# S5 mixer in channel-major form: 32-column output matmuls, half swaps and shifts as ACT copies, no folding transfers

## The chip, the core and the metric

The kernel runs on one core of a Trainium2 chip. Its engines are PE (TensorE, matrix products into PSUM; PEld in the profile is its weight load), DVE (VectorE, elementwise work), ACT (ScalarE, activations and copies), POOL (GpSimd) and SP (whose queue issues nearly all DMAs). The metric is the time of one execution in microseconds (us), the median of the runs. Lower is better.

## What is computed

Four layers on a 256 x 1024 activation: an even layer (stick-breaking attention and an S5 mixer, side by side), a gated linear attention layer, and two hybrid layers. The change touches the S5 mixer of the even layer alone:

```python
def s5_mixer(u, lam_re, lam_im, log_dt, b_re, b_im, c_re, c_im, d_skip, w_glu, b_glu):
    uf = u.reshape(bsz, L, S5_GROUPS, S5_GROUP)          # 32 groups of 16 channels
    lam_bar = exp(lam * dt)                              # 64 complex states a group
    b_bar = ((lam_bar - 1.0) / lam)[..., None] * bmat
    bu = einsum('gnp,blgp->blgn', b_bar, uf)             # complex
    h[t] = lam_bar * h[t - 1] + bu[t]                    # by associative_scan
    y = einsum('gpn,blgn->blgp', c_re, h.real) - einsum('gpn,blgn->blgp', c_im, h.imag) + d_skip * uf
    y = gelu(y.reshape(bsz, L, S5_WIDTH))
    return y * sigmoid(y @ w_glu + b_glu)
```

## The kernel before

Weights stream from HBM in 1 MB tiles (`Prog.loads`, raw, three buffers). ACT rounds each tile to an fp32r part (`highs`, whi), DVE makes the remainder (`lows`, wlo, four instructions of 512 columns a tile), and PE multiplies with both (`proj_a`, tile pa; `proj_b`, tile pb). whi and wlo have three buffers each, so DVE can run up to three tiles ahead of PE.

The order of the instructions on every engine is fixed when the program is built. Each part of the work is a generator, a fiber (`Prog.spawn`), and `Prog.run` takes again and again the fiber whose next instruction can start first by the planner's own table of costs (`Engine.__getattr__`) and a bias. On the chip each engine then works through its list in that order.

Even layer (`even_layer`): PE does the projections q, u, k, v, q, k, v, then z_b (ezb, two tiles), z_a (eza, four), the gate of the S5 mixer (eglu, `glu_evac`), and the output projection (eout, `out_proj`). `stick_fiber` (attention, PSUM tile sbz) and `s5_fiber` run beside them. The S5 mixer works on time in blocks: four steps are one block, so 64 blocks j of four steps t, and eight groups of 16 channels are one piece, so four pieces b. In `s5_piece`, piece by piece:

- ep: four transposes turn the table ez (made on DVE by `s5_tables`) into weights, which ACT copies to E twice, once with each of two 16-channel masks (g.half).
- inner: gp is a small product for the response within a block, G its masked form; four products with the shift matrices sh1 to sh3 and the identity shift G down by 32 partitions a step into tp, which ACT copies to Tt (s5T).
- vp: eight products of E with the input U; ACT copies vp to V. A product with the matrix jt swaps the halves of V (real and imaginary parts, with a sign) into jp. DVE turns V by the angles of the tables cosj and sinj, scans it, turns it back; the second turn has another product with jt.
- yp: per quarter q one product Tt[q] x U and two products F x m, which go to PSUM partitions 0 to 63 and 64 to 127. Rows of yp are (pair, step t, channel). ACT copies yp to Y.

All PE products of the S5 mixer are plain float32; the profile shows two records for each, one for each of its two passes. After the fourth piece `s5_fiber` folds Y into channel-major order with 32 DMAs on SP's queue (s_room<-s5Y), adds d_skip * u, and makes the gelu with ACT and DVE; y2 is split into the tile mix (`y_split`), which eglu reads. The input u is folded by 16 DMAs (s_room<-s_room, `u_evac`).

All instructions are emitted by one helper, so every line of the profile says L275; tiles are told apart by name. s_room is the shared tile that holds cosj, sinj, U and u.

Of the kernel before, what the change touches and what calls it, by code (L numbers as in the profile page):

```python
# [87 lines left out]
for _n, _w in _COLS:  # L88
# [4 lines left out]
    ["ident", "ones", "negtri", "negones", "mlt", "mneg", "cum", "mle", "jt", "misc", "sh1", "sh2", "sh3"])}  # L93
# [3 lines left out]
def _consts():  # L97
    i = np.arange(P)
    s, t = i[:, None], i[None, :]
    c = np.zeros((P, 13, P), np.float32)  # L100
# [8 lines left out]
    for m in range(64):  # L109
        c[m + 64, 8, m] = -1  # L110
        c[m, 8, m + 64] = 1
    c[:, 9, :64] = np.arange(64)
    c[:, 9, 65:] = 1
    for n in range(3):
        c[:, 10 + n] = s == t + 32 * (n + 1)
# [145 lines left out]
class Engine:  # L261
# [604 lines left out]
def program(g):  # L866
# [13 lines left out]
    c3 = A["cst"].rearrange("p (a b) -> p a b", a=13)  # L880
# [13 lines left out]
    def later():  # L894
        yield lambda: "later" in g.flags
        yield sp.dma_start(out=sgc, in_=A["cst2"][:, 1792:1796])
        yield sp.dma_start(out=g.cst1, in_=c3[:, 2:13, :])
        yield sp.dma_start(out=g.rsin.bitcast(I32), in_=A["pos"].to_broadcast([P, T]))
# [22 lines left out]
    with tc.tile_pool(name="blk1", bufs=1) as blk1:  # L921
        g.cst1 = blk1.tile([P, 11, P], F32, name="cst1")
# [157 lines left out]
def s5_tables(g, S):  # L1080

    act, dve, pool = g.act, g.dve, g.pool
    for b in range(4):
# [19 lines left out]
        own = lambda t: lambda a: t.rearrange("p (q a t c) -> p q a t c", q=4, t=4, a=2)[:, :, a]  # L1103
        F = yield from g.get("s5F", [P, 512])
        yield from s5_tab(g, bc, own(F), S.L[:, 0, gs, :], 2)
        yield from s5_tab(g, bc, own(m), S.L[:, 1, gs, :], 3)
        yield dve.tensor_tensor(F, F, m, op=OP.subtract)
        g.put(m, bc)
        S.fr[b] = (F, rho)


def s5_piece(g, S, Y, b):

# [11 lines left out]
    E = yield from g.get("s5E", [P, 4, 2, P])  # L1125
# [4 lines left out]
    Tt = yield from g.get("s5T", [P, 4, P])  # L1130

    def inner():
# [7 lines left out]
        tp = yield from g.ps1("proj", "s5tp")  # L1140
        tp4 = tp.rearrange("p (x t c) -> p x t c", x=8, t=4)
# [3 lines left out]
        g.put(tp, f0)  # L1145
# [6 lines left out]
    g.put(E)  # L1152
    if b == 3:
        g.flags.add("E")
    V = yield from g.get("s5V", [P, 512])
    yield act.activation(V, vp, AF.Copy)
    g.put(vp)
    jp = yield from g.ps1("small", "s5jp")
    yield pe.matmul(jp, g.K("jt"), V, start=True, stop=True)
# [5 lines left out]
    yield dve.tensor_tensor(r3(B)[:, :, 1:64], cb[:, :, 1:64], r3(V)[:, :, 0:63], op=OP.mult)  # L1165
    m = yield from g.get("s5m", [P, 512])
    yield dve.tensor_tensor(r3(m)[:, :, 1:64], sb[:, :, 1:64], r3(jp)[:, :, 0:63], op=OP.mult)
    g.put(jp)
    yield dve.tensor_tensor(r3(B)[:, :, 1:64], r3(B)[:, :, 1:64], r3(m)[:, :, 1:64], op=OP.subtract)
    if b not in S.fr:  # L1170
        yield lambda: b in S.fr
    F, rho = S.fr[b]
# [19 lines left out]
    g.put(F, m, Tt)  # L1192
    yield act.activation(Y[:, 4 * b:4 * b + 4, :], yp[:, 0:256].rearrange("p (q j) -> p q j", q=4), AF.Copy)
# [3 lines left out]
def s5_fiber(g, S):  # L1197
    act, dve, pool, sp, C = g.act, g.dve, g.pool, g.sp, g.C
    uT = S.uT
    Y = yield from g.get("s5Y", [P, 16, 64])  # L1200
    for b in range(4):
        yield from s5_piece(g, S, Y, b)

    yT = S.U.rearrange("p (b t) j -> p b t j", b=4)
    Y4 = Y.rearrange("p (b q) j -> p b q j", b=4)
# [10 lines left out]
    yf = S.U.rearrange("p b j -> p (b j)")
    for b in range(4):
        yb = yT[:, b].rearrange("p t j -> p (t j)")
        c = slice(b * T, (b + 1) * T)
        yield dve.scalar_tensor_tensor(yb, uT[:, b].rearrange("p t j -> p (t j)"), C("s5d", b), yb, op0=OP.mult, op1=OP.add)  # L1220
        yield act.activation(sq[:, c], yf[:, c], AF.Square)
    for h in range(2):
        c = slice(h * 512, (h + 1) * 512)
        yield dve.tensor_scalar(sq[:, c], sq[:, c], 0.044715, 1.0, op0=OP.mult, op1=OP.add)
        yield dve.tensor_tensor(gi[:, c], sq[:, c], yf[:, c], op=OP.mult)
        yield act.activation(gi[:, c], gi[:, c], AF.Tanh, scale=math.sqrt(2.0 / math.pi))

    for b in range(4):
        yield dve.scalar_tensor_tensor(y2[:, b].rearrange("p (j t) -> p t j", t=4),
                                       gi[:, b * T:(b + 1) * T].rearrange("p (t j) -> p t j", t=4),  # L1230
                                       1.0, yT[:, b], op0=OP.add, op1=OP.mult)
    g.put(S.room)
    g.flags.add("y2")
# [49 lines left out]
def even_layer(g, ev):  # L1283
# [723 lines left out]
```

## Time and profile before

| | |
|---|---|
| median of 3 runs | 1039.59 us (1039.35 to 1040.86) |
| profiled execution | 1040.25 us, span 1038.5 us |
| PE busy | 1016.1 us (98%) |
| DVE busy | 822.6 us (79%) |
| ACT busy | 564.4 us (54%) |
| granted TensorE clock | 0.998 of full |
| S5 pieces on PE | from 60.9 to 138.6 us |
| DMA, mean | 185 GB/s |

The span is cut in stretches with the view of windows; waits are read in the view of who waited for whom; prices of single steps are distances of starts in the timeline, since neighbouring matmuls overlap. A busy time is a union: the gap of a matmul's fill and drain is hidden in it.

### The profile page before, as it was taken

The page shows a single profiled execution, that of the slowest core. Times are in us where ns is not written, and L with a number is a line of the kernel's source. Part 1 is how long each engine was busy: PE and PEld are TensorE (multiplying, and loading weights), DVE is VectorE, ACT ScalarE, POOL GpSimd, SP SyncE. Part 2 cuts the span into 40 slices and gives each one's busy share as a digit, 9 for nine tenths or more (in the row PEclk, how much of TensorE's full clock was granted, in tenths as well). Part 3 has the DMA queues.
Part 4 walks back from the last instruction along what each step waited for, and adds up shares of the span by engine and source line. Part 5 has one row for each costly group of instructions (what it writes and reads, how often), then busy time and mean ns, then how long its engine had stood idle before and what let it go on. Part 6 is the DMA issues. An engine that isn't in the chain of part 4 may idle for free.

```text
span 1038.5 us, 14764 instructions
## 1 busy us (share of the span) xinstructions
PE 1016.1 (98%) x5507; PEld 857.5 (83%) x5507; DVE 822.6 (79%) x1855; ACT 564.4 (54%) x957; POOL 1.7 (0%) x15
## 2 busy tenths in 40 slices
PE   9999999899999999999999999999999999999996
PEld 7877888687887788888888888878888888888885
DVE  7998958777889777775799987775776759996775
ACT  6658667455744754544534564565454453365552
POOL 0000000000000000000000000000000000000000
PEclk9999999999999999999999999999999999999999
DMA  8543142545647486563533666544645454354541
GB/s 318 196 137 132 51 135 89 203 162 213 262 180 263 178 318 267 204 243 122 186 139 125 230 254 243 197 150 181 243 167 218 163 172 157 124 197 169 202 176 41
DMA packets 33491, 192.35 MB, mean 185 GB/s; under 512 B 8171, under 2 KB 9195, under 8 KB 11148
## 3 DMA queue, kind: packets, MB, share of 16 engines
q1 hardware_dynamic: 33132, 190.90, 51.2%
q8 instruction: 43, 0.70, 0.3%
q10 hardware_dynamic: 288, 0.52, 0.1%
q14 instruction: 28, 0.23, 0.1%
HBM read 189.31 MB, written 1.05 MB: 183 GB/s over the span
## 4 chain that ended last, share of the span: by engine, by line
PE 78%; DVE 13%; DMA 3%; ACT 2%; issue 2%; SPq 0%; DVEq 0%; ACTq 0%
PE pb L275 47%; PE pa L275 19%; DVE wlo L275 4%; PE as L275 3%; PE ret L275 2%; DMA raw<-in_wall_dram 2%; PE sbz L275 1%; DVE rs L275 1%; ACT whi L275 1%; DVE s5B L275 1%; PE s5yp L275 1%; PE gsc L275 1%; DVE s_room L275 1%; DMA cols<-in_cols_dram 1%; DVE H L275 0%
## 5 line engine op out<-in xcount | busy, mean ns | idle before, releaser
L275 PE MATMUL pb<-H,whi 128*128 128x512 f32 x1344 | 470.3, 401 | 1.2 <-ACT qsq L275 0.8
L275 DVE TENSOR_TENSOR wlo<-raw,whi 128x512 fp32r<-128x512 f32 x604 | 393.0, 687 | 93.2 <-ACT whi L275 93.2
L275 PE MATMUL pb<-H,wlo 128*128 128x256 f32 x1344 | 353.6, 283 | 0.0
L275 ACT ACTIVATE whi<-raw 128x1024 fp32r<-128x1024 f32 x302 | 304.6, 1052 | 69.2 <-PE pa L275 33.0
L275 PEld LDWEIGHTS pb<-H,whi 128*128 128x128 f32 x1344 | 242.6, 188 | 47.8 <-issue 1.5
L275 PEld LDWEIGHTS pb<-H,wlo 128*128 128x128 f32 x1344 | 253.5, 189 | 15.9 <-issue 0.7
L275 PE MATMUL pa<-whi,H 128*128 128x512 f32 x576 | 181.8, 394 | 2.1 <-DVE H L275 2.1
L275 PEld LDWEIGHTS pa<-whi,H 128*128 128x128 f32 x576 | 107.3, 188 | 26.2 <-DVE H L275 3.5
L275 PE MATMUL pa<-wlo,H 128*128 128x512 f32 x288 | 113.8, 395 | 0.0
L275 ACT ACTIVATE zz<-pb 128x256 f32<-128x256 f32 x120 | 45.0, 379 | 115.8 <-PE pb L275 115.2
L275 PE MATMUL pb<-yy,whi 128*128 128x512 f32 x192 | 67.6, 399 | 0.2
L275 DVE TENSOR_TENSOR zz<-pb,zz 128x256 f32<-128x256 f32 x120 | 49.8, 421 | 19.7 <-ACT zz L275 19.2
L275 DVE SCALAR_TENSOR_TENSOR acc<-raw,cact,acc 128x512 f32<-128x512 f32 x84 | 60.0, 747 | 4.6 <-DMA raw<-in_wall_dram 4.6
L275 PEld LDWEIGHTS pa<-wlo,H 128*128 128x128 f32 x288 | 54.1, 188 | 11.5 <-DVE wlo L275 0.3
L275 PE MATMUL pb<-yy,wlo 128*128 128x256 f32 x192 | 48.7, 281 | 0.0
L275 PE MATMUL pa<-whi,mg 128*128 128x512 f32 (+1 forms) x144 | 41.3, 369 | 0.0
L275 PEld LDWEIGHTS pb<-yy,whi 128*128 128x128 f32 x192 | 34.8, 188 | 7.3 <-DVE tg L275 1.5
L275 PEld LDWEIGHTS pb<-yy,wlo 128*128 128x128 f32 x192 | 36.2, 189 | 2.8
L275 PE MATMUL pa<-whi,mix 128*128 128x512 f32 x96 | 30.3, 393 | 3.0 <-ACT mix L275 2.3
L275 ACT ACTIVATE sqj<-x 128x512 f32<-128x512 f32 (+1 forms) x19 | 11.5, 606 | 37.1 <-DVE x L275 32.6
L275 PEld LDWEIGHTS pa<-whi,mg 128*128 128x128 f32 x144 | 26.0, 188 | 5.1
L275 ACT ACTIVATE ka<-pb 128x256 f32<-128x256 f32 x24 | 9.2, 385 | 37.4 <-PE pb L275 37.4
(289 smaller groups left out, 1142.7 us busy)
## 6 DMA issues: line engine op xcount, KB each, us to landing
raw<-in_wall_dram SPq DMA_DIRECT2D x174, 1024.0 KB, 4.8
x<-in_x_dram SPq DMA_DIRECT2D x2, 512.0 KB, 5.5
raw<-in_wall_dram SPq DMA_DIRECT2D x2, 512.0 KB, 5.8
s5bc<-in_s5bc_dram SPq DMA_DIRECT2D x4, 256.0 KB, 2.6
gate<-in_bgate_dram SPq DMA_DIRECT2D x2, 512.0 KB, 5.9
c<-in_cst_dram SPq DMA_DIRECT2D x1, 896.0 KB, 6.5
cst<-in_cst_dram SPq DMA_DIRECT2D x1, 704.0 KB, 11.7
s_room<-s_room SPq DMA_DIRECT2D x16, 32.0 KB, 4.5
```

Of the source, the lines that this page charges most:

```text
L275: i.eng, i.emit = name, (lambda: real(*a, **k))
```

## The change

- Outputs channel-major: for each step t the piece makes rows (quarter q, channel) of yp, 32 partitions for each q. Tt and F are padded with zeros to 32 columns (two groups of 16) and live in two fixed tiles S.Tt (s_T in the rows) and S.F (s_F), cleared once by POOL. The 12 matmuls of a piece become 48 of 128 x 32 weights and 64 columns, four neighbours writing to the four quarters of the PSUM partitions. Writers of both tiles wait for the flag ("yp", b - 1), set when the matmuls of the piece before are issued.
- Y, its four ACT copies and the 32 DMAs go; d_skip * u is added by DVE straight out of yp, per piece.
- The halves are swapped by two ACT copies of 64 partitions each (`turned`) instead of the product with jt; V is then the swapped copy and DVE reads vp itself.
- The shifts of G are six ACT copies (one of 128, one of 64 and four of 32 partitions, 128 columns each) instead of the four products with sh1 to sh3 and the identity and the copy of 512 columns. The constants jt, sh1, sh2, sh3 go: the second load of constants is 448 KB instead of 704 KB.
- Paired inputs: ACT masks U (two copies of 256 columns into EU) instead of E, and vp is four products with 128 columns instead of eight with 64.
- The subtraction that ends F is two instructions of 256 columns instead of one of 512.
- The gelu is made in two halves; the first half is a fiber of its own that starts in the fourth piece. y2 takes the buffer of E, z_b that of Y.
- The planner books 0.04 us for a matmul with an output of 32 partitions.

```diff
@@ cost table
                     i.cost = (0.4167 * n + 13.4) * 1e-3 if rhs.dtype == F32R else max(0.224, (1.667 * n + 4) * 1e-3)
+                    if chip[0][1].shape[0] == 32:
+                        i.cost = 0.04
@@ s5_tables
+        if b:
+            yield lambda: ("yp", b - 1) in g.flags
+        F = lambda a: S.F[:, :, a, :, 16 * a:16 * a + 16]
+        own = lambda a: m.rearrange("p (a q t c) -> p a q t c", q=4, t=4, a=2)[:, a]
...
-        yield dve.tensor_tensor(F, F, m, op=OP.subtract)
+        for a in range(2):
+            yield dve.tensor_tensor(F(a), F(a), own(a), op=OP.subtract)
@@ s5_piece
-    for a in range(2):
-        yield act.activation(E[:, :, a, :], ep.rearrange("p (q n) -> p q n", q=4), AF.Copy,
-                             scale=g.half[:, a:a + 1])
+    yield act.activation(EU[:, 0, :], ep, AF.Copy)
...
-        for tau in range(4):
-            yield pe.matmul(tp4[:, :, tau, :], g.K(f"sh{3 - tau}") if tau < 3 else g.ident, G, start=True, stop=True)
-        yield act.activation(Tt, tp.rearrange("p (q n) -> p q n", q=4), AF.Copy)
+        if b:
+            yield lambda: ("yp", b - 1) in g.flags
+        for tau, p0, n in ((3, 0, 128), (2, 32, 32), (2, 64, 32), (2, 96, 32), (1, 64, 64), (0, 96, 32)):
+            d = p0 - 32 * (3 - tau)
+            yield act.activation(Tt[d:d + n, :, tau, :], G3[p0:p0 + n], AF.Copy)
...
-    for i in range(8):
-        yield pe.matmul(vp[:, i * 64:(i + 1) * 64], E[:, i // 2, i % 2, :], U[:, 4 * b + i // 2, :], start=True, stop=True)
+    for a in range(2):
+        yield act.activation(EU[:, 1].rearrange("p (q a j) -> p q a j", q=4, a=2)[:, :, a, :], U[:, 4 * b:4 * b + 4, :], AF.Copy,
+                             scale=g.half[:, a:a + 1])
+    for q in range(4):
+        yield pe.matmul(vp[:, q * P:(q + 1) * P], EU[:, 0, q * P:(q + 1) * P], EU[:, 1, q * P:(q + 1) * P], start=True, stop=True)
...
+    def turned(o, v):
+        yield act.activation(o[0:64], v[64:128], AF.Copy, scale=-1.0)
+        yield act.activation(o[64:128], v[0:64], AF.Copy)
-    yield act.activation(V, vp, AF.Copy)
-    yield pe.matmul(jp, g.K("jt"), V, start=True, stop=True)
+    yield from turned(V, vp)
...
-    yield pe.matmul(jp, g.K("jt"), V, start=True, stop=True)
-    yield dve.tensor_tensor(m, jp, m, op=OP.add)
+    yield from turned(m, V)
+    yield dve.tensor_tensor(r3(B), cb, r3(B), op=OP.mult)
+    yield dve.tensor_tensor(m, m, B, op=OP.add)
...
-    for q in range(4):
-        yield pe.matmul(yp[:, q * 64:(q + 1) * 64], Tt[:, q, :], U[:, 4 * b + q, :], start=True, stop=False,
-                        skip_group_check=True)
+    for t in range(4):
+        o = lambda q: yp[32 * q:32 * q + 32, t * 64:(t + 1) * 64]
+        for q in range(4):
+            yield pe.matmul(o(q), Tt[:, q, t, :], U[:, 4 * b + q, :], start=True, stop=False, skip_group_check=True)
         for a in range(2):
-            i = 2 * q + a
-            yield pe.matmul(yp[64 * a:64 * a + 64, q * 64:(q + 1) * 64], F[:, i * 64:(i + 1) * 64], m[:, i * 64:(i + 1) * 64],
-                            start=False, stop=a == 1, skip_group_check=True)
-    yield act.activation(Y[:, 4 * b:4 * b + 4, :], yp[:, 0:256].rearrange("p (q j) -> p q j", q=4), AF.Copy)
+            for q in range(4):
+                i = 2 * q + a
+                yield pe.matmul(o(q), S.F[:, q, a, t, :], m[:, i * 64:(i + 1) * 64], start=False, stop=a == 1, skip_group_check=True)
+    g.flags.add(("yp", b))
+    yield dve.scalar_tensor_tensor(yb, S.uT[:, b].rearrange("p t j -> p (t j)"), g.C("s5d", b), yp[:, 0:T], op0=OP.mult, op1=OP.add)
@@ s5_fiber
-    for q in range(4):
-        for a in range(2):
-            for t in range(4):
-                yield (g.pool if t == 9 else sp).dma_start(out=yT[(2 * q + a) * 16:(2 * q + a) * 16 + 16, :, t, :],
-                                                        in_=Y4[a * 64 + t * 16:a * 64 + t * 16 + 16, :, q, :])
+    yield from gelu(1)
+    yield from g.join(S.first)
```

How the lists move, at three places. First PE, the output matmuls of piece 0 (s5T, s_T: response within a block; s5F, s_F: output table). Before:

```order
L275 MATMUL qtp<-cst_76,qraw 128x128
L275 MATMUL s5yp<-s_room,s5T 128x64
L275 MATMUL s5yp<-s5m,s5F 64x64 x2
L275 MATMUL s5yp<-s_room,s5T 128x64
L275 MATMUL s5yp<-s5m,s5F 64x64 x2
```

After:

```order
L269 MATMUL s5yp<-s_room,s_T 32x64 x4
L269 MATMUL pa<-wlo,H 128x512
L269 MATMUL pa<-whi,H 128x512
L269 MATMUL s5yp<-s5m,s_F 32x64 x8
L269 MATMUL s5yp<-s_room,s_T 32x64 x4
L269 MATMUL s5yp<-s5m,s_F 32x64 x8
```

The pair "one full-width, two half-width" comes four times before; now four rounds of four and eight quarter-width matmuls, with other matmuls put in behind the first four (so in pieces 0, 1 and 3; piece 2 has none).

Second ACT, between the first vp and the next table (s5E now holds EU; s5f is G and later the next f0). Before:

```order
L275 ACTIVATE s5E<-s5ep,sgc 128x4x128
L275 ACTIVATE vE<-pa 128x512
L275 ACTIVATE s5V<-s5vp 128x512
L275 ACTIVATE s5T<-s5tp 128x512
L275 ACTIVATE s5f_845<-s5bc,sgc 128x128
```

After:

```order
L269 ACTIVATE s5E<-s5ep 128x512
L269 ACTIVATE s5E<-s_room,sgc 128x4x64 x2
L269 ACTIVATE vE<-pa 128x512
L269 ACTIVATE s_T<-s5f_162 128x4x32
L269 ACTIVATE s5V<-s5vp 64x512 x2
L269 ACTIVATE s_T<-s5f_162 32x4x32 x3
L269 ACTIVATE s_T<-s5f_162 64x4x32
L269 ACTIVATE s_T<-s5f_162 32x4x32
L269 ACTIVATE s5f_840<-s5bc,sgc 128x128
```

The four S5 copies up to G (the first of E stands two rows higher) have become eleven. Over the whole list ACT has 33 instructions more, three of them loads of an activation table (14 instead of 11).

Third DVE, from the sum out of the last yp to the first part of mix that eglu reads. After the change:

```order
L269 SCALAR_TENSOR_TENSOR s_room<-s_room,cols,s5yp 128x256
L269 TENSOR_TENSOR zz<-pb,zz 128x256
L269 TENSOR_TENSOR wlo<-raw,whi 128x512
L269 TENSOR_SCALAR s_room<-s_room 128x512
...
L269 TENSOR_TENSOR wlo<-raw,whi 128x512 x3
L269 TENSOR_TENSOR zz<-pb,zz 128x256
L269 SCALAR_TENSOR_TENSOR y_1654<-s_room 128x4x64 x2
L269 TENSOR_TENSOR gz<-gz,oT 128x512 x2
L269 SCALAR_TENSOR_TENSOR mix<-y_1654,mix 128x256
```

From that sum to the fourth `mix<-y` the list has 30 DVE instructions. On PE the last yp stood before the z_b tiles, in the last v projection; now piece 2 stands among the z_b tiles and piece 3 in the z_a tiles, 34 pb pairs, 6 sbz products with constants and 12 with vE before the first eglu matmul. DVE's list up to the last `mix<-glt` of the even layer is four instructions longer and has as many `wlo` as before (96); the lists of the layers behind it are the same on PE.

## Rows read from the trace of the kernel before

**Rows 1.** Page, part 1: busy time and share of the span, instructions

```profile
PE 1016.1 (98%) x5507; PEld 857.5 (83%) x5507; DVE 822.6 (79%) x1855; ACT 564.4 (54%) x957; POOL 1.7 (0%) x15
```

**Rows 2.** Windows: length, busy per engine (x instructions), clock, DMA share, GB/s

```profile
57.44:203.00 145.56, 139.98 (x816) 113.45 (x814) 124.73 (x270) 98.81 (x181) 1.28 (x8) 1.00 0.38 128
188.00:203.00 15.00, 11.18 (x48) 8.22 (x48) 13.55 (x24) 7.98 (x16) 0.61 (x2) 1.00 0.64 230
203.00:230.00 27.00, 26.59 (x121) 21.73 (x121) 17.05 (x37) 14.27 (x22) 0.00 (x0) 1.00 0.34 123
```

**Rows 3.** Waits of PE, 57.44 to 230: total, times, longest

```profile
PE pa L275 <- ACT mix L275: 2.3, 1, 2.3
PE pb L275 <- DVE zz L275: 1.1, 2, 0.7
```

**Rows 4.** Timeline of PE: start, us, instructions; first vp, swap and shifts

```profile
64.78 2.00 PE L275 MATMUL s5vp<-s_room,s5E 128*128 128x64 f32 x16
66.61 0.36 PE L275 MATMUL s5gp<-s5f,s5ez 128*128 128x32 f32 x2
...
67.59 1.02 PE L275 MATMUL s5jp<-s5V,cst 128*128 128x512 f32 x2
68.44 1.05 PE L275 MATMUL s5tp<-s5f,cst 128*128 128x128 f32 x8
69.25 0.47 PE L275 MATMUL pa<-wlo,H 128*128 128x512 f32 x1
```

**Rows 5.** Timeline of PE, the first yp

```profile
77.63 0.35 PE L275 MATMUL s5yp<-s_room,s5T 128*128 128x64 f32 x2
77.91 0.34 PE L275 MATMUL s5yp<-s5m,s5F 128*64 128x64 f32 x4
78.17 0.43 PE L275 MATMUL s5yp<-s_room,s5T 128*128 128x64 f32 x2
...
80.06 0.55 PE L275 MATMUL qtp<-cst,qraw 128*128 128x128 f32 x3
```

**Rows 6.** Weight loads of the first yp: tile view (min/median/max ns), then timeline

```profile
L275 PEld LDWEIGHTS s5yp<-s5m,s5F x64: 132/134/136, 77.9 to 138.3; 128*64 128x64 f32 x64
...
77.90 0.20 PEld L275 LDWEIGHTS s5yp<-s5m,s5F 128*64 128x64 f32 x4
...
78.17 0.30 PEld L275 LDWEIGHTS s5yp<-s_room,s5T 128*128 128x128 f32 x2
```

**Rows 7.** Waits of DVE, 57.44 to 203

```profile
DVE wlo L275 <- ACT whi L275: 6.2, 4, 4.5
DVE zz L275 <- ACT zz L275: 5.9, 2, 3.4
...
DVE s5m L275 <- PE s5jp L275: 1.5, 3, 0.6
```

**Rows 8.** Tile view of F: DVE instructions

```profile
L275 DVE TENSOR_TENSOR s5F<-s_L,s5bc x8: 418/430/468, 61.7 to 124.0; 128x256 f32<-128x256 f32 x8
L275 DVE TENSOR_TENSOR s5F<-s5F,s5t x4: 682/700/735, 65.5 to 125.6; 128x512 f32<-128x512 f32 x4
```

**Rows 9.** The start: ACT in the timeline, and the load of constants

```profile
26.43 2.01 ACT L275 ACTIVATE whi<-raw 128x1024 fp32r<-128x1024 f32 x2 [0.81 <-DMA raw<-in_wall_dram]
...
cst<-in_cst_dram SPq DMA_DIRECT2D x1, 704.0 KB, 11.7
```

**Rows 10.** ACT: the copy of vp (tile view), the table load (group, mean ns)

```profile
L275 ACT ACTIVATE s5V<-s5vp x4: 585/594/598, 66.8 to 127.6; 128x512 f32<-128x512 f32 x4
...
L275 ACT ACT_TABLE_LOAD x11 | 14.1, 1283 | 0.9 <-PEq L1997 0.7
```

**Rows 11.** Chain that ended last, in order of time: stretches of PE

```profile
103.49 3.60 PE sbz L275 x12
...
108.60 2.73 PE sbz L275 x24
...
144.67 9.04 PE pb L275 x51
```

More of the change, by code (lines that the diff above doesn't have):

```diff
@@ L92 @@
 CST = {n: i for i, n in enumerate(
-    ["ident", "ones", "negtri", "negones", "mlt", "mneg", "cum", "mle", "jt", "misc", "sh1", "sh2", "sh3"])}
+    ["ident", "ones", "negtri", "negones", "mlt", "mneg", "cum", "mle", "misc"])}
 def _consts():
@@ L108, in _consts @@
     c[:, 7] = s <= t
[L109 to L115, printed above, removed]
+    c[:, 8, :64] = np.arange(64)
     c2 = np.zeros((P, 1796), np.float32)
@@ L896, in later @@
         yield sp.dma_start(out=sgc, in_=A["cst2"][:, 1792:1796])
-        yield sp.dma_start(out=g.cst1, in_=c3[:, 2:13, :])
+        yield sp.dma_start(out=g.cst1, in_=c3[:, 2:9, :])
         yield sp.dma_start(out=g.rsin.bitcast(I32), in_=A["pos"].to_broadcast([P, T]))
@@ L1148, in s5_piece @@
         yield g.on("u")
+    for a in range(2):
+        yield act.activation(EU[:, 1].rearrange("p (q a j) -> p q a j", q=4, a=2)[:, :, a, :], U[:, 4 * b:4 * b + 4, :], AF.Copy,
+                             scale=g.half[:, a:a + 1])
     vp = yield from g.ps1("small", "s5vp")
-    for i in range(8):
-        yield pe.matmul(vp[:, i * 64:(i + 1) * 64], E[:, i // 2, i % 2, :], U[:, 4 * b + i // 2, :], start=True, stop=True)
-    g.put(E)
+    for q in range(4):
+        yield pe.matmul(vp[:, q * P:(q + 1) * P], EU[:, 0, q * P:(q + 1) * P], EU[:, 1, q * P:(q + 1) * P], start=True, stop=True)
+    g.put(EU)
     if b == 3:
-        g.flags.add("E")
+        S.y2 = yield from g.get("s5E", [P, 4, T], name="y2")
+        S.first = g.spawn(S.gelu(0), 0.1)
+    def turned(o, v):
+        yield act.activation(o[0:64], v[64:128], AF.Copy, scale=-1.0)
+        yield act.activation(o[64:128], v[0:64], AF.Copy)
     V = yield from g.get("s5V", [P, 512])
-    yield act.activation(V, vp, AF.Copy)
-    g.put(vp)
-    jp = yield from g.ps1("small", "s5jp")
-    yield pe.matmul(jp, g.K("jt"), V, start=True, stop=True)
+    yield from turned(V, vp)
     cb, sb = S.cosj[:, gs, :], S.sinj[:, gs, :]
@@ L1164, in s5_piece @@
     yield pool.memset(r3(B)[:, :, 0:1], 0.0)
[L1165 to L1169, printed above, removed]
+    yield dve.tensor_tensor(r3(B)[:, :, 1:64], cb[:, :, 1:64], r3(vp)[:, :, 0:63], op=OP.mult)
+    g.put(vp)
+    yield dve.tensor_tensor(r3(V)[:, :, 0:63], sb[:, :, 1:64], r3(V)[:, :, 0:63], op=OP.mult)
+    yield dve.tensor_tensor(r3(B)[:, :, 1:64], r3(B)[:, :, 1:64], r3(V)[:, :, 0:63], op=OP.subtract)
     if b not in S.fr:
         yield lambda: b in S.fr
-    F, rho = S.fr[b]
+    rho = S.fr[b]
     yield dve.tensor_tensor_scan(B, rho.rearrange("p a j -> p (a j)"), B, 0.0, OP.mult, OP.add)
@@ L1175, in s5_piece @@
     yield dve.tensor_tensor(r3(V), sb, r3(B), op=OP.mult)
-    yield dve.tensor_tensor(r3(m), cb, r3(B), op=OP.mult)
-    g.put(B)
-    jp = yield from g.ps1("small", "s5jp")
-    yield pe.matmul(jp, g.K("jt"), V, start=True, stop=True)
-    g.put(V)
-    yield dve.tensor_tensor(m, jp, m, op=OP.add)
-    g.put(jp)
+    m = yield from g.get("s5m", [P, 512])
+    yield from turned(m, V)
+    yield dve.tensor_tensor(r3(B), cb, r3(B), op=OP.mult)
+    g.put(V)
+    yield dve.tensor_tensor(m, m, B, op=OP.add)
@@ L1216, in s5_fiber @@
[L1216 to L1231, printed above, removed]
+    act, dve = g.act, g.dve
+    gw = S.cosj.rearrange("p a j -> p (a j)")
+    yf = S.U.rearrange("p b j -> p (b j)")
+    def gelu(h):
+        y2 = S.y2
+        sq, gi = gw[:, 1024 * h:1024 * h + 512], gw[:, 1024 * h + 512:1024 * h + 1024]
+        y = yf[:, 512 * h:512 * h + 512]
+        yield act.activation(sq, y, AF.Square)
+        yield dve.tensor_scalar(sq, sq, 0.044715, 1.0, op0=OP.mult, op1=OP.add)
+        yield dve.tensor_tensor(gi, sq, y, op=OP.mult)
+        yield act.activation(gi, gi, AF.Tanh, scale=math.sqrt(2.0 / math.pi))
+        for b in range(2):
+            c = slice(b * T, (b + 1) * T)
+            yield dve.scalar_tensor_tensor(y2[:, 2 * h + b].rearrange("p (j t) -> p t j", t=4), gi[:, c].rearrange("p (t j) -> p t j", t=4),
+                                           1.0, y[:, c].rearrange("p (t j) -> p t j", t=4), op0=OP.add, op1=OP.mult)
@@ L1232, in s5_fiber @@
+    S.gelu = gelu
+    for b in range(4):
+        yield from s5_piece(g, S, b)
+    yield from gelu(1)
+    yield from g.join(S.first)
     g.put(S.room)
@@ L1409, in even_layer @@
             sticks.append(g.spawn(stick_fiber(g, qk, oT, hf, pr), -0.05))
-    if "E" not in g.flags:
-        yield g.on("E")
-    zb = yield from g.get("s5E", [P, 4, T], name="zb")
+    zb = yield from g.get("s5Y", [P, 4, T], name="zb")
     for j in range(2):
```

45 lines of the change are left out of this document (18 added, 27 removed).

## The prediction

> **What bounds the kernel now.** I read the page's busy times first: PE is busy 98% of the span, DVE 79%, ACT 54% [rows 1]. So time taken from PE counts, as long as another engine doesn't step into its place. That has to be read from the stretch of the S5 mixer, not from the mean, so the windows come second. From the first S5 table on DVE (57.44 us) to DVE's last product for the gate of the S5 mixer (203.0) the stretch is 145.56 us long; PE is busy for 139.98 of it, DVE for 124.73, ACT for 98.81 [rows 2]. PE is ahead by 15 us only, much less than on the page. The waits of PE come third: it loses 5.6 us in the stretch (145.56 - 139.98), of which 2.3 and 1.1 are its two largest waits, at the end, for parts of mix and for zz [rows 3]. In the last 15 us before 203 DVE is busy for 13.55, PE for 11.18 only [rows 2]. DVE is the next bound, and the end of this layer already belongs to it. Behind 203 PE is busy for 26.59 of 27 us and DVE for 17.05 [rows 2]; what is gained at 203 should reach the end, where PE's list is the same.
>
> **PE, piece by piece.** Prices are distances of starts.
> - The two products with jt: the first takes 67.59 to 68.44, 0.85 us [rows 4]. Two a piece: -1.70.
> - The shifts: 68.44 to 69.25, -0.81 [rows 4].
> - vp: 16 records from 64.78 to 66.61, 1.83 us [rows 4]. It becomes 8 records with full-width weights and 128 columns, the form of the shifts, whose 8 records take 0.81: -1.02.
> - yp: 24 records from 77.63 to 80.06, 2.43 us [rows 5]. It becomes 96 records, that is 12 sets of four matmuls that write to four different quarters. No row shows a set, so I bound it. Below: 512 columns passed twice take 0.85 us [rows 4], so 64 columns twice take 0.11, and four side by side no less: 12 x 0.11 = 1.3 us. Above, as long as they run in twos like the half-width ones: two of those take 0.26 (77.91 to 78.17), a change of width there and back with it [rows 5], so 24 x 0.26 = 6.2 us. I take 0.15 a set, near the low end: the four half-width loads of two matmuls last 0.20 us together and 0.134 each, so the last begins 0.07 behind the first, where two full-width loads (0.30 together) begin 0.11 apart [rows 6]. Neighbours in different columns run side by side, and within the new loop the width doesn't change. That is 1.8. One change of width there and back is added: a quarter of the old loop lasts 0.61, of which two full-width records are 0.23 (1.83 / 8) and two half-width matmuls side by side 0.11, which leaves 0.27. In all 2.1: -0.3.
>
> Together -3.83 a piece, -15.3 for four. In three pieces the order puts other matmuls in behind the first four of yp: three more changes of width, +0.8. PE: **-14.5**, to 125.5 us in the stretch. The transposes and gp stay.
>
> The Trainium skill (TensorEngine Tiling, Instruction Overhead) speaks against small pieces: each matmul carries some 60 cycles, so that few columns cost as much as 60, and the gain of tiling shouldn't be taken from a dimension that is small already. By that, at the 2.4 GHz that the granted clock of 1.00 means, an estimate from the page is 96 x 0.025 = 2.4 us of overhead a piece, 2.7 with the change of width, and PE would gain 12.1 instead of 14.5. The half-width loads of rows 6, four begun in 0.07 us, speak for less than that.
>
> **DVE** does the same work: turn, scan and sums keep count and size, d_skip and gelu too. Only the end of F is cut: two of 430 ns for one of 700 [rows 8], +0.16 a piece, +0.6, so 125.4 us. So DVE stands level with PE, and the sum goes by DVE: 125.4 us and its waits. It has 20.8 us without work now (145.56 - 124.73). Of these, 6.2 and 5.9 are waits for whi and zz [rows 7]: whi had no free buffer and zz no finished product, so PE's pace made them, and a faster PE takes them away. Of the other 8.7, the 1.5 for the product with jt [rows 7] go. I keep 7 for what is left: sbz, tables, and now ACT's swaps. Stretch: 125.4 + 7 = 132.4 instead of 145.56, **-13.2**. The bounds are 0 us of waits (-20.2) and 12 (-8.2). PE then waits some 7 us in the stretch, mostly late.
>
> **ACT** gets more: per piece 13 copies instead of five, none longer than the 594 ns of a 512-column copy from PSUM [rows 10], so below +5 us a piece, and three table loads of 1283 ns [rows 10], +3.9. Even that bound makes 98.8 + 24 = 123 us, below 132. As work it is hidden by PE and DVE; without that cover it would cost those 24 us. As a wait it counts: DVE and PE stand behind each swap, and a swap can stand behind a pair of whi (2.01 us, rows 9). That is in the 7.
>
> **Edits that cost nothing.** The 32 DMAs of Y and its four copies (ACT) go from a tail that PE covers with the z projections. SP issues its weight loads without them in between; no wait of PE names them. POOL's two clears come before any table, on an engine with 1.7 us of work [rows 1]. The flags "yp" change little: the old single buffers of F and Tt made the same wait.
>
> **The start.** The load of constants falls from 704 KB [rows 9] to 448. Weight tiles queue behind it, and ACT waits 0.81 us for one at 26.43 [rows 9]. A gain between 0 and 0.8; I take **-0.2**, since DVE is busy soon after whatever PE does.
>
> **Sum.** -13.2 - 0.2 = -13.4 us against the profiled execution's own 1040.25: 1026.9. That execution stands 0.7 above the median of the runs (1039.59), so I forecast **1026** for the median. With DVE's bounds this case runs from 1019 to 1031.
>
> **Rivals.**
> 1. *The S5 chain comes too late for its gate.* Pieces 2 and 3 have moved from the v projections to the z tiles. Between the last yp and eglu PE has 34 pairs of pb (68 records; 51 take 9.04, so 12.1) and sbz of 3.60 and 2.73 [rows 11], 18.4 us. DVE has 30 instructions there, at the pace of the last 15 us (13.55 / 24, rows 2) 16.9 us. So only 1.5 us are free: what DVE is behind PE at the last yp beyond that, PE waits before eglu. For it: the two are level in the sum. Against it: eglu starts with the first quarter of mix. If DVE's waits are 13 instead of 7, the gain is 7.4 and the time about 1032; the case runs from 1031 to 1036.
> 2. *PE can't begin records fast enough (the other side).* Place: yp. The old loop's 24 records in 2.43 us are 0.10 each [rows 5]; if no stream goes faster, 96 records are 9.7 us, 10.0 with the change of width, +7.6 instead of -0.3, so +4.0 a piece and +16: PE's stretch 156 and its 5.6 of waits, **1055**. It decides from (2.43 + 3.53 - 0.27) / 96 = 0.059 us a record: above that the change loses on PE. For it: no stretch of records in rows 4 and 5 is denser than 0.10. Against it: four loads begun in 0.07 us [rows 6].
> 3. *The same, at the break-even*: about 0.06 a record, PE is even and the time stays near 1039. The Trainium skill has a figure for that (TensorE: Matmul & The Clock Gate, "Wait — 56ns, not 53.3ns?"): 62 ns for each matmul that the sequencer decodes in its own code, which binds where the array's work is shorter. Whether it binds here no row shows: all streams in the rows have longer work.
>
> That the change doesn't do what it says is out: the order has no jp, tp or Y left and 48 quarter-width matmuls a piece.
>
> **Chances.** Forecast 0.61, late chain 0.27, break-even 0.06, slower 0.06. A measurement of this kernel tells 0.2%, about 2 us. Faster is 0.61 + 0.27 = 0.88, same 0.06, slower 0.06. The range from 1020 to 1035 leaves out the last two (0.12) and thin ends of the first two. It takes in DVE's waits from 1 to 10 us and the late chain nearly whole.
>
> **What would show it.** A yp of about 2 us, up to 2.7 at the skill's estimate, would bear the price out; above 5.7 a piece refutes it. From DVE's first table to its last `mix<-glt` I expect 132 us, DVE over 93% busy, PE near 125. PE's waits should be at eglu and in the output projection, 7 us together; over 12 before eglu is rival 1. Behind that the two traces should run in step, 13 us apart. If DVE's waits fall on swaps (ACT) instead, the copies were too cheap in my sum. The forecast is wrong if DVE's share stays near 86% while PE's falls.

## The result, and the profile after

The changed kernel takes **1027.66 us** (median of 4 runs, 1025.53 to 1028.51); the kernel before takes 1040.01 in the same comparison (4 runs, 1039.35 to 1040.86). The ratio is 0.9878, 95% interval 0.9860 to 0.9895: 12.4 us faster, forecast 1026. The profiled execution of the changed kernel is its fastest, 1025.53 us, span 1023.7, so the two traces stand 14.8 us apart, 2.4 more than the medians. One of the six executions of the run with more matmuls behind yp (below) ran at a granted clock of 0.849 and took 1106.43 us; its median is given without that one.

The page's busy times after, against [rows 1]:

```profile
PE 998.8 (98%) x5715; PEld 846.2 (83%) x5715; DVE 823.6 (80%) x1859; ACT 581.0 (57%) x990; POOL 3.0 (0%) x17
```

PE has 17.3 us less work, DVE 1 more, ACT 16.6 more; PE's idle time has grown from 22.4 us (1038.5 - 1016.1) to 24.9. The windows after: the stretch of the prediction (first table on DVE to its last `mix<-glt`), its last 15 us, and the 27 us behind it, with the columns of [rows 2]:

```profile
55.99:186.84 130.85, 121.88 (x1016) 101.33 (x1015) 124.66 (x274) 114.30 (x214) 1.29 (x8) 0.99 0.38 134
171.84:186.84 15.00, 11.27 (x48) 9.10 (x47) 13.81 (x24) 10.27 (x18) 0.61 (x2) 0.89 0.39 144
186.84:214.00 27.16, 26.75 (x122) 21.90 (x121) 15.85 (x37) 13.39 (x22) 0.00 (x0) 1.00 0.42 155
```

The stretch is 14.7 us shorter. DVE is busy for 95% of it (before 86%), PE for 121.88 us, ACT for 114.30. The waits of PE after, from the first table to 214 us, against [rows 3]:

```profile
PE pb L269 <- DVE zz L269: 3.7, 1, 3.7
PE sbz L269 <- ACT sb_sp L269: 1.1, 1, 1.1
PE s5yp L269 <- ACT s_T L269: 1.1, 1, 1.1
PE sbz L269 <- DVE sb_sp L269: 0.9, 1, 0.9
PE s5yp L269 <- DVE s5m L269: 0.8, 2, 0.4
```

The largest lies in the gate of the S5 mixer. Two timelines show it, PE and then DVE:

```profile
173.87 0.40 PE L269 MATMUL pb<-mix,whi 128*128 128x512 f32 x1
178.00 0.50 PE L269 MATMUL pb<-mix,whi 128*128 128x512 f32 x1 [3.73 <-DVE zz L269]
...
180.08 0.63 PE L269 MATMUL pa<-whi,mix 128*128 128x512 f32 x1
180.51 0.63 PE L269 MATMUL pa<-wlo,mix 128*128 128x512 f32 x1
...
182.21 0.62 PE L269 MATMUL pa<-whi,mix 128*128 128x512 f32 x2
182.67 0.40 PE L269 MATMUL pa<-wlo,mix 128*128 128x512 f32 x1
```

```profile
170.90 3.09 DVE L269 TENSOR_TENSOR wlo<-raw,whi 128x512 fp32r<-128x512 f32 x5
174.19 0.69 DVE L269 SCALAR_TENSOR_TENSOR gz<-gz,zz 128x512 f32<-128x512 f32 x1 [0.20 <-ACT gz L269]
...
177.52 1.08 DVE L269 TENSOR_TENSOR zz<-pb,zz 128x256 f32<-128x256 f32 x3
```

PE wants a PSUM buffer at 174.3 us; DVE frees it with the zz at 177.52. Before that DVE had spent 3.09 us on five remainders for the output projection, which starts at 180. But they don't hold it up: behind them it still waits 0.20 us for gz from ACT. ACT's timeline shows why that gz is late:

```profile
169.93 0.39 ACT L269 ACTIVATE zz<-pb 128x256 f32<-128x256 f32 x1 [0.40 <-PE pb L269]
170.21 2.00 ACT L269 ACTIVATE whi<-raw 128x1024 fp32r<-128x1024 f32 x2
172.23 1.28 ACT L269 ACT_TABLE_LOAD   x1
173.53 0.64 ACT L269 ACTIVATE gz<-zz 128x512 f32<-128x512 f32 x1
```

Between the zz of the z_a tiles and gz stand two roundings for the output projection and the load of an activation table. From gz to the zz that frees the buffer, DVE and ACT take turns. So the wait belongs to both lists.

The wait costs more than itself. Windows of the 3.5 us behind it and of the next 3.8:

```profile
178.69:182.21 3.52, 3.52 (x11) 2.85 (x10) 2.75 (x5) 2.27 (x5) 0.00 (x0) 0.52 0.01 5
182.21:186.00 3.79, 3.79 (x18) 3.12 (x17) 3.79 (x7) 2.23 (x4) 0.30 (x1) 1.00 0.00 0
```

After PE stood still for 3.73 us its granted clock is 0.52, the 1.2 GHz level, and a matmul of 512 columns takes 0.43 us (180.08 to 180.51); at 1.00 it takes 0.23 (two from 182.21 to 182.67). For the ten that begin in the stretch, seven of 512 and three of 256 columns, that is an estimated 1.5 us more, which the page books as busy.

The new operations. PE's timeline of piece 2, whose yp nothing interrupts, and of the first vp; then ACT's copies in the tile view (min/median/max ns):

```profile
63.13 1.05 PE L269 MATMUL s5vp<-s5E 128*128 128x128 f32 x8
63.94 0.47 PE L269 MATMUL pa<-wlo,H 128*128 128x512 f32 x1
...
129.00 0.32 PE L269 MATMUL s5yp<-s_room,s_T 128*32 128x64 f32 x8 [1.07 <-ACT s_T L269]
129.13 0.41 PE L269 MATMUL s5yp<-s5m,s_F 128*32 128x64 f32 x16
129.36 0.29 PE L269 MATMUL s5yp<-s_room,s_T 128*32 128x64 f32 x8
...
130.14 0.41 PE L269 MATMUL s5yp<-s5m,s_F 128*32 128x64 f32 x16
130.47 0.39 PE L269 MATMUL pb<-H,wlo 128*128 128x256 f32 x1
```

```profile
L269 ACT ACTIVATE s_T<-s5f x24: 294/309/313, 64.2 to 143.1; 32x128 f32<-32x128 f32 x16, 128x128 f32<-128x128 f32 x4, 64x128 f32<-64x128 f32 x4
...
L269 ACT ACTIVATE s5m<-s5V x8: 617/632/633, 75.2 to 147.2; 64x512 f32<-64x512 f32 x8
```

vp takes 0.81 us, as booked. A whole yp takes 1.47 us (129.00 to 130.47) instead of 2.43 [rows 5]: a round of twelve matmuls 0.34 us, a set of four 0.112, a record 0.014.

### The profile page after: what moved, and what is told of

Read it like the earlier page. It is cut to its first block, busy times and chain, and to the rows that moved or that the text cites. A ratio compares the mean times of both kernels' runs of the same rounds, so it can differ in the third digit from the quotient of the medians.

```text
span 1023.7 us, 15184 instructions
## 1 busy us (share of the span) xinstructions
PE 998.8 (98%) x5715; PEld 846.2 (83%) x5715; DVE 823.6 (80%) x1859; ACT 581.0 (57%) x990; POOL 3.0 (0%) x17
## 4 chain that ended last, share of the span: by engine, by line
PE 81%; DVE 9%; ACT 6%; issue 2%; DMA 1%; SPq 0%; DVEq 0%; ACTq 0%
PE pb L269 49%; PE pa L269 20%; PE as L269 4%; DVE wlo L269 3%; PE ret L269 2%; ACT whi L269 1%; PE sbz L269 1%; DVE rs L269 1%; ACT L269 1%; PE ntp L269 1%; PE gsc L269 1%; DMA raw<-in_wall_dram 1%; ACT sb_sp L269 1%; ACT s_room L269 1%; DMA cols<-in_cols_dram 0%
## 5 line engine op out<-in xcount | busy, mean ns | idle before, releaser
L269 DVE TENSOR_TENSOR zz<-pb,zz 128x256 f32<-128x256 f32 x120 | 49.9, 421 | 14.5 <-ACT zz L269 14.1
```

The costliest lines, as they stand in the source:

```text
L269: i.eng, i.emit = name, (lambda: real(*a, **k))
```

## The experiments

To compare the layer in all kernels I use one window that begins and ends on PE: from the first transposes for the S5 mixer (ep) to the last matmul of the output projection. What lies behind it is 808.5 us in both traces. Row by row before, the changed kernel, and the runs below, columns as above:

```profile
60.88:229.95 169.07, 163.56 (x922) 133.02 (x922) 138.29 (x289) 110.55 (x200) 1.28 (x8) 1.00 0.38 127
```

```profile
59.42:215.15 155.73, 146.74 (x1127) 121.99 (x1128) 138.23 (x293) 125.77 (x233) 1.29 (x8) 0.99 0.38 134
```

So PE has 16.8 us less to do in it, and 9.0 instead of 5.5 us without work; DVE has the same 138 us.

**Theory at the start:** DVE sets the end of the layer now, and PE has time to spare. **Rival:** PE still sets it, and every us on PE counts.

### More matmuls behind yp, more DVE work

```diff
+        for n in range(12):
+            for q in range(4):
+                c = 256 + n % 4 * 64
+                pe.real.matmul(yp[32 * q:32 * q + 32, c:c + 64], Tt[:, q, n % 4, :], U[:, 4 * b + q, :], start=True, stop=True,
+                               skip_group_check=True)
```

> The changed kernel with 48 more quarter-width matmuls behind the output matmuls of each piece (products of s_T with U, into columns of the same PSUM bank that nobody reads); every list keeps its order, only these are put in. At the 0.112 us that a set of four took in the changed kernel they are 4 x 12 x 0.112 = 5.4 us of PE. Theory (DVE sets the end of the even layer): PE has 9 us without work in the stretch and waits 3.7 us before the gate for DVE, so the 5.4 us come for the most part out of that wait: between -1 and +2 us against the changed kernel, 1026.5 to 1030. Rival (PE still sets the end): +5.4 us, about 1033.

Measured 1036.35 us (median of five), ratio 0.9962 (0.9950 to 0.9974), 8.7 us above the changed kernel. Neither expectation covers that. In the trace PE stops in the added bursts for nothing that the profile names. Its timeline, then the window behind the first hole:

```profile
82.31 0.39 PE L1200 MATMUL s5yp<-s_room,s_T 128*32 128x64 f32 x10
84.92 1.43 PE L1200 MATMUL s5yp<-s_room,s_T 128*32 128x64 f32 x86 [2.23 <-issue]
```

```profile
86.28:89.95 3.67, 3.67 (x16) 3.08 (x12) 1.80 (x5) 2.14 (x10) 0.00 (x0) 0.54 0.11 41
```

There are three such holes, two in the bursts (2.2 and 1.2 us) and one right behind the last (1.4), 4.8 us in all, beside the 5.4 us of work; and the granted clock falls to 0.54 behind the first. So the run says too much as a price of PE time; but the work itself isn't free here.

```diff
+    yield also(i, first=lambda: [dve.real.tensor_tensor(S.pad, S.pad, S.pad, op=OP.add) for _ in range(2)])
```

> The changed kernel with two more DVE instructions of 512 columns (0.60 us each, on a tile of their own) ahead of the sum out of yp in each piece; order otherwise the same. 8 x 0.60 = 4.8 us of DVE. Theory (DVE sets the end of the even layer): +4 to +5 us, about 1032, and PE's wait before the gate grows from 3.7 to about 8 us. Rival (PE sets the end, DVE only keeps pace): less than +1 us, about 1028.

Measured 1029.64 us, ratio 0.9889 (0.9876 to 0.9902). That is 2.0 us above the changed kernel. A kernel with the changed kernel's order in the same comparison (the constants, below) had 1026.46; against that it is +3.2. By the ratios it is 1.1 and 2.8. In the trace, the window of the layer and the stretch behind PE's wait for zz:

```profile
59.64:219.34 159.70, 148.21 (x1127) 122.72 (x1128) 143.01 (x301) 125.75 (x233) 1.29 (x8) 0.98 0.37 131
181.30:186.60 5.30, 5.30 (x15) 4.33 (x16) 3.90 (x8) 3.41 (x8) 0.00 (x0) 0.50 0.08 34
```

The window is 4.0 us longer for 4.8 us more DVE work. The other side is the changed kernel's fastest execution, and part of it is the clock: PE needs 148.21 us for the same 1127 records (146.74 in the changed kernel), since the stretch at the lower level lasts 5.3 us here. So DVE's time costs something, but "paid in full" is not shown. PE's wait for zz stayed 3.7; the new waits of PE are in the pieces, so that part of the expectation failed.

### yp quarter by quarter

```diff
-    pairs = [[(q, t) for q in range(4)] for t in range(4)]
+    quarter = [[(q, t) for t in range(4)] for q in range(4)]
```

> The changed kernel with its 48 output matmuls of a piece in another order: all twelve of one quarter of the PSUM partitions behind each other, then the next quarter; the count, the sizes and all other places stay. Theory (a set costs 0.112 us because four neighbours run side by side in different column groups): a matmul alone takes that 0.112 us, so 48 take 5.4 us instead of 1.35, +16 us of PE in four pieces, of which some 4 to 6 are taken by PE's waits: +10 to +12 us, about 1038. Rival (records are short in themselves, at 0.014 us each, whatever quarter they write): no change, 1027.7.

Measured 1038.42 us, ratio 0.9969 (0.9959 to 0.9979). PE's timeline:

```profile
82.06 0.91 PE L269 MATMUL s5yp<-s5m,s_F 128*32 128x64 f32 x13
...
83.24 0.89 PE L269 MATMUL s5yp<-s5m,s_F 128*32 128x64 f32 x13
...
84.38 0.89 PE L269 MATMUL s5yp<-s5m,s_F 128*32 128x64 f32 x13
```

Twelve matmuls now take 1.14 us instead of 0.34, 12.8 us more in sixteen rounds. So the cheap yp comes from neighbours in different quarters, as expected. The time rises by 10.8 to 12.0 us (against the changed kernel and against its order in the same comparison; by the ratios 9.5 and 11.1): of the 12.8 little disappears in waits, where 4 to 6 of 16 were expected to. PE's wait for zz stayed (3.9). DVE's waits name the path:

```profile
DVE s_F L269 <- PE s5yp L269: 7.2, 3, 2.6
```

The next table F waits for the yp of the piece before, which still reads the only buffer; the changed kernel's trace names no such wait. DVE stands in front of it, with all that is queued behind. So yp is a link of a loop through the pieces (table, vp, scan, yp, next table), and my theory was that PE time in that loop is paid in full, though DVE is the busier engine. The windows up to the end of the last yp, the changed kernel and this run, name a simpler rival:

```profile
59.42:150.50 91.08, 87.14 (x841) 73.12 (x842) 86.51 (x193) 82.12 (x161) 0.68 (x6) 1.00 0.38 133
```

```profile
60.53:164.00 103.47, 100.37 (x841) 86.68 (x842) 89.78 (x197) 83.17 (x162) 0.68 (x6) 1.00 0.36 120
```

PE had only 3.9 us without work there (91.08 - 87.14). Of 12.8 us more at least 8.9 had to be paid in these pieces wherever they lay, loop or not. The theory led to the next run.

### PE work outside the loop

```diff
+                if k == 0 and key[0] in ("eza", "ezb"):
+                    twice = lambda wh=wh, hl=hl, both=both: [pe.real.matmul(both, wh, hl, start=True, stop=True) for _ in range(2)]
+                    yield also(pe.matmul(both, wh, hl, start=True, stop=False), first=twice)
```

> The changed kernel with the first product of every accumulation in the z_b and z_a tiles issued three times instead of once (the first two results are overwritten): 24 more of 0.235 us, 5.6 us of PE that no part of the S5 mixer waits for; order otherwise the same. Theory (the even layer's end is set by DVE and by the loop through the pieces: tables on DVE wait for the output matmuls of the piece before): PE's time outside that loop is nearly free, 0 to +2 us against the changed kernel, and PE's wait of 3.7 us before the gate shrinks. Rival (PE's time is paid in full wherever it lies): +5 to +6 us.

Measured 1027.81 us, ratio 0.9879 (0.9864 to 0.9894): 0.2 us above the changed kernel and 1.4 above the 1026.46 of its order, no difference clear of the noise, for 5.6 us of matmuls. One execution's window is 2.1 us longer, with PE busy for 4.2 us more, at the edge of what was expected:

```profile
59.98:217.77 157.79, 150.91 (x1152) 126.35 (x1152) 138.28 (x293) 125.67 (x233) 1.30 (x8) 0.99 0.38 132
```

So PE's time in the z tiles is paid in part at most: by the medians 0.2 to 1.4 us of it, by this trace half. That fits the loop and the simpler rival alike, since the work went into idle time that PE had; no run tells the two apart. Nor do the medians show DVE's 4.8 us to be dearer than PE's 5.6: the two intervals (0.9876 to 0.9902, 0.9864 to 0.9894) overlap. The wait for zz was 3.9 us here; PE's spare time was taken from the waits in the pieces.

### Parts undone

The swaps by products again (PE +6.8 us, sixteen ACT copies less):

```diff
-    yield from turned(V, vp)
+    yield act.activation(V, vp, AF.Copy)
+    yield pe.matmul(jp, g.K("jt"), V, start=True, stop=True)
...
-    yield from turned(m, V)
+    yield pe.matmul(jp, g.K("jt"), V, start=True, stop=True)
```

> The changed kernel with one part undone: the halves are swapped by the product with jt again (two products and two PSUM tiles a piece, one copy of vp; the sixteen half-width ACT copies go). The planner places it anew. Theory (PE time is paid in full, about two thirds of DVE's): 4 x 1.7 = 6.8 us of PE come back, +5 to +7 us, about 1033. Rival (the swaps on ACT cost as much in waits as the products did on PE): within 2 us of the changed kernel, 1026 to 1029.

Measured **1024.41 us**, ratio 0.9844 (0.9826 to 0.9861): not slower, rather 2 to 3 us faster, though the intervals just touch (the changed kernel's begins at 0.9860). Both expectations fall.

```profile
59.65:214.58 154.93, 152.16 (x1143) 123.82 (x1144) 138.10 (x293) 115.19 (x219) 1.50 (x8) 1.00 0.38 135
```

The largest wait of PE is now:

```profile
PE pa L272 <- ACT mix L272: 0.7, 1, 0.7
```

PE works 5.4 us more in the window and stands idle for 2.8 us instead of 9.0; the wait for zz is gone, and the clock stays at 1.00. The order gives a reason: the pieces come earlier, so the last yp stands 136 PE instructions ahead of the gate, in the changed kernel 87. ACT's last table load before the gate stands at 140.44 us there, not at 172.23. These products lie in the loop too, and their 5.4 us are not paid: they take the place of ACT copies in the same loop. Which share the shorter ACT list has in the gain, and which the planner's luck, one run doesn't tell.

With the shifts and vp undone as well (the diff of the change backwards; the output form, the gelu in halves and the absent folding stay):

> The changed kernel with three parts undone: swaps by the product with jt, shifts by products, vp as eight products with masked tables. What stays is the channel-major output of the pieces (48 quarter-width matmuls), the sum out of PSUM, the gelu in halves and the absent folding transfers. Against the kernel with only the swaps undone (1024.4 us, PE idle for 2.8 us from the first transposes to the output projection) PE gets 4 x (1.0 + 0.8) = 7.3 us more. Theory (with the swaps back PE is at its bound there): +4 to +7 us, 1028 to 1031. Rival (these parts are worth nothing either, the output form made the whole gain): 1024 to 1026.

Measured 1034.51 us, ratio 0.9939 (0.9926 to 0.9951), slower than expected. In the trace the window grows by 7.1 us for the 7.3 booked:

```profile
59.43:221.49 162.06, 159.35 (x1210) 130.62 (x1210) 140.09 (x293) 110.46 (x195) 1.29 (x8) 1.00 0.37 129
```

PE idles for 2.7 us again: down to here PE is the bound. The medians of these two differ by 10.1 us, their profiled executions by 7.8 only; the one profiled here was the fastest of six.

Only the second swap by a product, the first by copies out of vp:

> The changed kernel with only the second swap of a piece (after the scan) made by the product with jt again; the first stays as two ACT copies out of vp, which replace a copy that is needed anyway. Against the changed kernel PE gets 4 x 0.85 = 3.4 us more, ACT 4 x 1.26 = 5.0 us less; against the kernel with both swaps on PE, PE gets 3.4 us less and ACT 2.4 us more. The last output matmuls stand 134 PE rows ahead of the gate, as with both swaps on PE (136), and not 87 as in the changed kernel. Theory (DVE's list and the loop of the pieces set the layer's end, PE is level with it): as fast as with both swaps on PE or up to 3 us faster, 1021.5 to 1024.5, and PE's wait for zz before the gate is gone. Rival (PE's time is what counts): between the two, 1025 to 1027.

Measured 1024.78 us, ratio 0.9843 (0.9828 to 0.9857), as with both on PE:

```profile
60.48:214.50 154.02, 148.89 (x1135) 122.34 (x1136) 138.07 (x293) 119.67 (x224) 1.28 (x8) 1.00 0.39 136
```

PE has 3.3 us less to do than with both products and the window is 0.9 shorter. PE's wait for zz is 0.9 us. So from 154 to 156 us the window no longer follows PE. These two are the fastest kernels measured.

### Work taken off DVE, and the order

The subtractions that end the tables on POOL, order kept (`pool.real.tensor_tensor` in place of DVE's, twelve instructions):

> The changed kernel with the twelve subtractions that end the S5 tables (four of 512 columns, eight of 256) on POOL instead of DVE; every other instruction stays in its place. DVE gets 4 x 0.60 + 8 x 0.34 = 5.1 us less. Theory (DVE and PE are level and drag each other, 4.8 us more on DVE cost about 3): -1.5 to -3 us. Rival (DVE's time was only paid where it was added in the chain of a piece): within 1 us. A third outcome: POOL is slower than DVE by more than the tables' lead, and pieces wait: slower by some us.

Measured 1029.77 us, ratio 0.9890 (0.9872 to 0.9908), 2.1 us above the changed kernel, with overlapping intervals; the theory's gain didn't come. DVE was spared nothing: its busy time in the window is 138.50 us against 138.23, without the twelve. POOL's and DVE's timelines:

```profile
97.25 5.05 POOL L1099 TENSOR_TENSOR s5ez<-s5ez,s5t 128x512 f32<-128x512 f32 x1 [10.95 <-DVE s5t L275]
```

```profile
101.13 1.25 DVE L275 TENSOR_SCALAR rs<-qss 128x8 f32<-128x8 f32 x1
```

One of POOL's four subtractions of 512 columns needed 5.05 us while DVE worked beside it (the others 1.3 to 1.6), and a DVE instruction that takes 0.16 us elsewhere took 1.25 next to it. So this run doesn't test a lighter DVE.

The remainders held back until the last z_a evacuation, and ACT's rounding ahead of them:

```diff
+            if key == ("eout", 0, 1):
+                yield self.on(("za", 3))
```

> The changed kernel with one piece of the order moved: ACT's rounding of the second output-projection tile (2.0 us) and DVE's five remainders ahead of the last z_a evacuation (3.1 us), which had 12 us of lead, go behind it; all lists are the same up to there. Theory (PE's wait of 3.7 us before the gate is DVE's and ACT's list between the last sum out of yp and the gate, with work in it that isn't due): the last gz starts 2 us earlier, PE's wait falls to about 1.7 us, and less of the clock is lost behind it: -2 to -3.5 us. Rival (the wait is set by the matmuls and products ahead of it, or comes back as a wait for the remainders behind it): within 1 us.

Measured 1025.78 us, ratio 0.9857 (0.9840 to 0.9874); the changed kernel's own order gave 0.9862 and 0.9878, so no difference is shown. The wait fell as worked out, and came back:

```profile
PE pb L269 <- DVE zz L269: 1.8, 1, 1.8
PE pa L269 <- ACT mix L269: 1.8, 1, 1.8
```

The first wait shrank because ACT's two roundings no longer stand ahead of gz (172.47 us instead of 173.53): DVE, without its remainders, waits 1.29 us for that gz. DVE's work is only moved: the second wait is for parts of mix that DVE and ACT make behind the remainders.

Rotary tables behind the gate (`yield g.on("glu")`), and k scaled by ACT:

> The changed kernel with work taken off DVE in the layer: the rotary tables (2.9 us on DVE, two loads of an activation table on ACT; first read at 497 us) start only behind the gate, and the four scalings of the transposed k (0.755 us each) are done by ACT. DVE gets 5.9 us less ahead of the gate, ACT 2.4 us more there less the two loads. Theory (DVE sets the end, ACT has 30 us without work): -3 to -6 us, 1021 to 1024. Rival (the loop of the pieces or PE sets it): within 1.5 us of the changed kernel.

Measured 1031.99 us, ratio 0.9917 (0.9902 to 0.9931): slower, though DVE has less to do. The planner moved the pieces: the last yp starts at 164.6 us instead of 150.1, and PE idles for 10.7 us in the window. Its 1127 records on PE take 151.95 us instead of 146.74: behind waits of 1.81 and 0.81 us for mix the granted clock is 0.50 from 193.2 to 198 us. This run doesn't test DVE's price, since the order changed with it.

The planner's price at 0.028 us:

> The changed kernel with the planner's price of a quarter-width matmul at the measured 0.028 us (0.112 / 4) instead of 0.04; what is computed and how is the same, the order differs from piece 1 on. It shows how much the order alone is worth: theory, within 3 us of the changed kernel either way; rival, the 0.04 is what made the gain, and the time rises by over 5 us.

Measured 1029.05 us, ratio 0.9886 (0.9867 to 0.9905): the 0.04 didn't make the gain. The last yp comes at 155.3 us. The order alone is worth one to three us.

### The constants

Four unused matrices back (704 KB), order kept:

> The changed kernel with four unused matrices put back behind the constants, so that the second load of constants is 704 KB again; order the same, and the planner is told the smaller size. Theory (the 256 KB less are what brought the first table on DVE from 57.4 to 56.0 us): the first table goes back to 57.4 us and the time rises by up to 1.4 us. Rival (the start differs by other things, the order of DVE and ACT or the weight tiles): less than 0.3 us.

Measured 1026.46 us, ratio 0.9862 (0.9849 to 0.9875): no difference. The first table starts at 56.37 us; it starts between 55.8 and 57.1 in the kernels with the changed order. The load is not what brought it forward from 57.44.

## Why the prediction was right

- **The sum by DVE** held. Forecast: DVE 125.4 us and 7 of waits, stretch 132.4. Measured: 124.66 and 6.2, stretch 130.85. DVE's share was to be over 93% and is 95%. That DVE sets this floor is argued, not shown: no run makes the layer shorter by less DVE work (on POOL nothing was spared, held back it was moved, and with the rotary tables the order changed).
- **Part of the near hit is luck.** Against the traces the stretch gave 1.5 us more than booked and the start 1.2 more; 1.4 were lost again behind the last `mix<-glt`, from which the output projection's end is 28.31 us away instead of 26.95. So the profiled execution lies 1.4 under the sum's 1026.9. The median lies 2.1 above that execution, where before it lay 0.7 below.
- **PE** was booked at -14.5 us; the page shows -17.3, with some 1.5 lost again to the clock. The mis-sized term is yp. I took 0.15 us a set and 2.1 us a piece; it is 0.112, the lower bound, and 1.47, which is 2.5 us for four. Estimate and measurement differ here: by the Trainium skill (TensorEngine Tiling (Array Packing), Instruction Overhead) I had estimated 2.7 us a piece; the trace has 1.47. With 0.014 us a record in four quarters and 0.048 in one, the costs of neighbours in different quarters don't add up. vp (0.81 booked, 0.81 measured) was right, and jt fits: undone it gives PE 5.4 us of the 6.8, with the clock's 1.5 saved.
- **PE's waits** were to be 7 us, at the gate and in the output projection. They are 9.0 in the stretch, 3.7 of them at the gate and none over 0.4 in the output projection; the others lie in the pieces.
- **Rivals 2 and 3** (a limit on beginning records) are refuted: their break-even is 0.059 us a record, the trace has 0.014, and even in one quarter 1.14 / 24 = 0.048. The 62 ns that the Trainium skill gives for a matmul that the sequencer decodes in its own code (TensorE: Matmul & The Clock Gate, "Wait — 56ns, not 53.3ns?") doesn't bind in this kernel: it is a figure for a matmul, which has two records here and takes 0.028 us.
- **Rival 1** (the S5 chain late for its gate) happened in small: 1.5 us were free, and PE waits 3.7 there. The late part is not DVE's pace, by which the rival was priced, but ACT's list ahead of gz. It did not reach the 12 that would have made it the likeliest.
- **What PE has to spare is worth nothing:** "the sum goes by DVE" said so, and the runs show it: the window is 162.06 us with PE busy for 159.35, 154.93 with 152.16, and then 154.02 and 155.73 with 148.89 and 146.74. So by these traces about 7 us of the window come from the output form and the absent folding (169.07 to 162.06) and 7 from vp and shifts (162.06 to 154.93); by the ratios it is 6 and 10. The output form, booked at -0.4 on PE (four times -0.3, and +0.8), gives 4.2 there (163.56 to 159.35), and 2.8 of PE's idle time go with it. The swaps, -1.70 a piece, the largest of my terms on PE, bring nothing.
- **"The flags yp change little"** was right: DVE waits for no yp in the changed kernel's trace. But the room is small: with the slower yp the same flag cost DVE 7.2 us.
- **ACT** got 15.2 us in the window (110.55 to 125.77), below the 24 of the bound. "As a wait it counts" holds: DVE waits 1.3 us for a first swap (below) and 0.4 for a second, PE 1.1 for a shift. What the sum hid as work, a table load of 1.28 us, stands on the chain to the gate.

```profile
DVE s5B L269 <- ACT s5V L269: 1.3, 1, 1.3
```

- **The start** gave 1.45 us (57.44 to 55.99) where I took 0.2. The load isn't its cause; what is stays open.
- Behind the output projection both traces run in step (808.5 us), 14.8 apart where I expected 13.

## What to carry to other kernels

- When two engines stand level, price PE time by the idle time of the stage where it lies: 12.8 us more in pieces with 3.9 us to spare were paid nearly whole, 5.6 us in the z tiles hardly. A gain past the point where the window stops following PE buys nothing. Undo the parts of a change singly: one of them may cost nothing to leave out, or be better left out.
- Small matmuls are cheap if neighbours write to different quarters of the PSUM partitions; the order of the loop decides that, here by a factor of three.
- A wait that the profile puts down to one engine can come from the list of another: follow the waits of the engine that it names. Holding back work that isn't due shortens such a wait, but only pays if the engine has time for it later.

## What the runs showed of the hardware

- Quarter-width float32 matmuls of 64 columns: 0.014 us a record with neighbours in four quarters, 0.048 within one.
- ACT's copies across partitions cost by columns: 309 ns for 128 columns, on 32, 64 or 128 partitions, 632 ns for 512 on 64.
- Behind a wait of PE of 3.73 us its granted clock was 0.52 for a stretch of 3.5 us, then 1.00 again. With two more DVE instructions a piece, the same wait (3.7 us) was followed by 5.3 us at 0.50; behind the wait of 1.8 us with the remainders held back, 512 columns took 0.23 to 0.25 us from the third matmul on, as at 1.00.
- DVE and POOL can hold each other up: once in twelve POOL took 5.05 us for an instruction that otherwise takes 1.3 to 1.6. The Trainium skill (SBUF — State Buffer, "SBUF: two separate sides") has a pair of ports that POOL, or a DVE instruction with two inputs in SBUF, holds for a whole instruction while the other blocks; the remainders beside that subtraction have two such inputs, so the row agrees.
- Bursts of 96 more such records behind the 96 of a yp stopped PE for up to 2.2 us without a releaser; in the changed kernel no such hole is over 0.3 us. Its cause wasn't tried.
